# A hybrid decoder layer on one core: the order of each engine's instructions, made by the frame's other machine model

## The chip, the cores and the metric

The kernel runs on one core of one Trainium2 chip. The metric is the device time of one execution in microseconds (us), lower is better. The five engines that matter are TensorE (PE, with its weight loads shown apart as PEld), VectorE (DVE), ScalarE (ACT), GpSimd (POOL) and SyncE (SP), whose queue issues the transfers here. Every engine carries out its own list of instructions in order; engines wait for one another through semaphores.

## The reference, cut to what matters

One layer on 1024 tokens of width 1024, all in float32:

```python
h = h + 0.5 * swiglu(rmsnorm(h, ffn1_norm), w_gate, w_up, w_down)          # D_FF = 2816
z = rmsnorm(h, mix_norm) @ w_in
m_qk, m_v, m_o, m_if, f_q, f_k, f_v, f_f = split(z)
m_qk = silu(causal_depthwise_conv(m_qk, conv_qk))
h_m = mlstm_chunkwise(heads(m_q), heads(m_k), heads(m_v), i_gate, f_gate)  # 4 heads, a state carried from chunk to chunk
y_m = head_rmsnorm(h_m, mlstm_out_norm) * sigmoid(m_o)
h_f = forgetting_attention(heads(f_q), heads(f_k), heads(f_v), f_gate)     # 8 heads, causal softmax, "FoX"
y_f = head_rmsnorm(h_f, fox_out_norm)
h = h + concat([y_m, y_f]) @ w_out
h = h + 0.5 * swiglu(rmsnorm(h, ffn2_norm), ...)
gate = sigmoid(rmsnorm(h, ple_gate_norm) @ w_ple_gate)
h = h + gate * rmsnorm(p @ w_ple_proj, ple_proj_norm)
return rmsnorm(h, final_norm)
```

## The kernel before, in words

**Arithmetic.** Every large product is made of three products of float32r halves (`mm3`, L94 to L98: hi by hi, lo by hi, hi by lo). A number is split into its halves by `split_from` (L100 to L103): a cast on ScalarE gives hi, a subtraction on VectorE (or GpSimd) gives lo. A product tile is 128 rows by 512 columns, one PSUM bank.

**Stages, in the order of the program.** (1) p @ w_ple_proj (`pp` in `ple_rows`, `ph`/`pl` are the halves of p) beside the first norms. (2) The first SwiGLU: its up and gate products `pp` in a Winograd form of seven block products for each of 11 pairs of dff tiles, then its down products `dn`. (3) The mixer's projections and gates, then the mLSTM (`mlstm`, L831 to L1010), chunk by chunk of 128 tokens: `d` (L921, L924) and its exponential `E` on ScalarE (L927), `st` (L935) and `PT`, the two pairs of heads `num` (L951, L953), the update `dl` of the state `C` (L956, L964), then the norm: `dn`, `sq`, `ss`, `r` (GpSimd, L107), `ysb` (L981). `back` (L1000) transposes the finished heads. A chunk's `num` needs the state of the chunk before. PSUM has two buffers for `num`, one for `d` and `dl` together. (4) FoX (`fox`, L1026 to L1257): scores `sc` (L1111 to L1114), their maximum `mx`, the exponential `pr` (ScalarE, L1123), transposes `tr` (L1161) and their halves `th`/`tl` (L102, L103), value products `ot` (L1141), the sum `O` (L1148, L1149); for each pair of heads and half of the tokens `finish` (transposes L1193, `sq`, `ss`, `v`, `r`, `yn`, transposes L1211), and `put_y` (L1013 to L1023) stores the halves into `yD` in DRAM. (5) `out_f` (L1287 to L1306) loads `yfh`/`yfl` from `yD` (L1295) and adds their products with w_out to `h`. (6) The second SwiGLU, and `embed` (`g` products, sigmoid, final norm).

**What sets the order.** The code is written in the wanted order. `weave(main, fill, frac)` (L605 to L622) emits two generators so that `fill` gets `frac` of the TensorE time that `main` counts: the mLSTM chunks are woven with the projection of the output gate (`pj`, L1010, 0.9), the attention with the projections of the later head pairs and `out_m` (`acc`, L1257, 1.13). Products of `fill` need nothing that `main` has just made; below they are called filler. `later`/`tick` put a value product three steps behind its transposes. What the code emits is collected by the frame, `tile.TileContext` (L1507), which places buffers and semaphores and then makes the list of each engine by a model of the machine: an instruction is put where the model finds it ready, so the lists can differ from the code's order. In the kernel before, TensorE's list follows the code nearly row by row. SP's queue carries all loads and stores of the kernel.

Of the kernel before, what the change touches and what calls it, by code (L numbers as in the profile page):

```python
# [14 lines left out]
PSUM = bass.MemoryType.PSUM  # L15
# [9 lines left out]
# pairs of dff tiles, and the order of the seven block products of a Winograd form  # L25
# [4 lines left out]
class Net:  # L30
# [26 lines left out]
    def raw_cols(self, w, c0):  # L57
        """128 columns of a [1024, N] weight: row k * 128 + p at [p, k]."""
        r = self.rp.tile([P, KT, P], F32, tag="raw", name="raw")
        self.nc.sync.dma_start(out=r, in_=w[:, c0:c0 + P].rearrange("(k p) n -> p k n", p=P))  # L60
        return r
# [6 lines left out]
    def split(self, raw, pool=None, tag="w", aside=False):  # L68
        """raw = hi + lo, both in float32r."""
        pool = pool or self.wp  # L70
        shape = list(raw.shape)
        hi = pool.tile(shape, F32R, tag=tag + "hi", name=tag + "hi")
        lo = pool.tile(shape, F32R, tag=tag + "lo", name=tag + "lo")
        self.split_from(hi, lo, raw, aside)
        return hi, lo

    def split2(self, raw, aside=False):
        """The two halves of k of a weight tile, each (hi, lo)."""
# [14 lines left out]
    def mm3(self, out, ahi, alo, bhi, blo, first, last):  # L93
        """out (+)= a.T @ b with a = ahi + alo and b = bhi + blo."""  # L94
# [5 lines left out]
    def split_from(self, hi, lo, src, aside=False):  # L100
        """src (PSUM or SBUF) = hi + lo; aside: on GpSimd (SBUF only)."""
# [8 lines left out]
    def norm_rows(self, src, gain, dst):  # L110
        """dst = RMSNorm(src) * gain for 128 tokens; dst also takes the squares."""
# [7 lines left out]
    def xunit(self):  # L119
        """Four k tiles by 512 columns, (hi, lo)."""  # L120
        return tuple(self.xp.tile([P, 4, 512], F32R, tag=t, name=t) for t in ("xhi", "xlo"))

    def new_xt(self):
        """[half of the tokens][half of the k tiles] -> (hi, lo)"""
        return [[self.xunit() for _ in range(2)] for _ in range(2)]

    def normer(self, src, gain, dst):
        """RMSNorm of one token tile after another, transposed and split into dst(i) -> (hi, lo).
        Returns step(i), which takes token tile i and finishes the one before; step.rows(i) only takes it,
        step.next() only finishes the oldest."""  # L130
# [31 lines left out]
    def wino_put(self, B, name, rows, i):  # L162
        """512 columns of token tile i, transposed, into a right operand."""
# [10 lines left out]
    def wino_normer(self, src, gain, B, rows, bufs):  # L174
        """RMSNorm of one token tile after another into the right operands of the seven products
        (x transposed: rows k < 512 and k >= 512, columns t < 512 and t >= 512, Winograd's form).
        Three operands wait in DRAM for wino_rest. step(i) takes token tile i and finishes the one
        before, step.last() finishes the last."""
# [43 lines left out]
    def wino_rest(self, B, name):  # L222
        """One of the operands that wait in DRAM, through its place for lo."""
# [9 lines left out]
    def swiglu(self, B, w_gate, w_up, pools):  # L233
        """hidD = silu(x @ w_gate) * (x @ w_up), transposed, by pairs of dff tiles; the products of a
        pair (2 x 2 blocks: dff tile, half of k, half of the tokens) in Winograd's form with seven
        block products, each of three float32r products."""
# [3 lines left out]
        def pair(m, which, s):  # L240
            """Appends the seven products of the dff tiles m, m + 1."""
# [13 lines left out]
            # the first pair's tile a is loaded again for the sums  # L255
# [18 lines left out]
            def slot(r, c):  # L274
                """Where block (dff tile r, token half c) is put together."""
# [7 lines left out]
            def out(r, c, x, y, t):  # L283
                """Block (r, c) is x + y."""
# [8 lines left out]
            def hidden(r, c):  # L293
                """The left operands of the product with w_down: A11 = H00, A12 = H10, A21 = H01, A22 = H11
                (H: dff tile, half of the tokens), S1 = A21 + A22, S2 = S1 - A11, S3 = A11 - A21, S4 = A12 - S2."""
# [58 lines left out]
            # block (0, 0) = P1 + P2, (0, 1) = P1 + P6 + (P5 + P3), (1, 1) = P1 + P6 + P7 + P5,  # L354
            # (1, 0) = P1 + P6 + P7 + P4 (T4 is negated)
# [3 lines left out]
        for m in range(0, DFF // P, 2):  # L359
            s = {}  # L360
            g, u = pair(m, 0, s), pair(m, 1, s)
            # the first products don't need the second half of the tokens, those after them not T2, T3, T4
# [20 lines left out]
    def down(self, h, w_down, hook):  # L383
        """h += 0.5 * hid @ w_down in Winograd's form (2 x 2 blocks: half of the tokens, parity of the dff
        tile, half of the columns), one of the seven products after the other. Yields after the first loads
        and after the first operands; hook(j, q) runs after pair q of product j (the last one in two parts,
        4 and 8, of 256 tokens each)."""
# [20 lines left out]
        def fetch(j, q):  # L408
            """The left operands of two pairs."""
# [11 lines left out]
        def prep(n):  # L421
# [19 lines left out]
            # in place: T1 = B12 - B11, T3 = B22 - B12, T2 = B22 - T1, T4 = B21 - T2  # L441
# [18 lines left out]
        with tc.tile_pool(reuse_waits="tile", name="dn", bufs=1, side="right") as dn, \  # L460
# [11 lines left out]
            def evict(j, i):  # L472
                """Returns what can wait."""
# [18 lines left out]
            # C11 = P1 + P2, C12 = P1 + P6 + P5 + P3, C22 = P1 + P6 + P7 + P5, C21 = P1 + P6 + P7 + P4  # L492
            # (T4 is negated)
# [22 lines left out]
    def ffn(self, h, gain, w_gate, w_up, w_down, norms, hook, bufs, early=False, release=None):  # L516
        """h += 0.5 * SwiGLU(RMSNorm(h)); norms(step, prepare, products, pools, load_gain) runs the normalization
        over the token tiles, prepare() has the first weights split; early: products(n) may run there."""
# [39 lines left out]
    def ple_rows(self, p, w_proj, ps):  # L558
        """ppD = p @ w_proj; yields after every product of 128 tokens by 512 columns."""
# [45 lines left out]
def weave(main, fill, frac):  # L605
    """Emit main and fill so that they advance together: fill gets frac of main's TensorE time.
    Both yield that time in us, or None where the one has to wait for the other."""
# [17 lines left out]
def proj_stream(N, w, xt, jobs, bank=None, begun=None, aside=False):  # L625
    """jobs: (column or raw tile, sink(half, psum), ready or None); the weights are split one tile ahead.
    begun: the weights of the first job, whose first half is done (its sink gets None)."""
# [34 lines left out]
class Mix:  # L662
# [5 lines left out]
    def consts(self, pool):  # L668
        """Masks, selectors and the per-channel parameters as columns."""
# [9 lines left out]
        # rows 0-15: conv taps (tap, tile), 16-19 mlstm_out_norm, 20-23 fox_out_norm  # L679
# [9 lines left out]
    def begin(self, xt):  # L689
        """The gates and the first projection for the first half of the tokens, into DRAM; yields  # L690
        after the weights and then between products."""
# [24 lines left out]
    def gates(self, xt, keep, gp, bank):  # L716
        """Yields between its steps, with about the time that VectorE takes."""
# [17 lines left out]
        # log sigmoid(x) = min(x, 0) - ln(1 + exp(-|x|))  # L735
# [6 lines left out]
        # sums within chunks of 128  # L742
# [8 lines left out]
        # mLSTM rows 0-3: m, r = b - m, e = i - b  # L751
# [15 lines left out]
        # hi rows at 0-3, lo rows at 32-35, zeros between: one product with a 0/1 selector adds them  # L767
# [20 lines left out]
        # token-major: [:, chunk, (e, ws, exp(-m)), head]  # L788
# [8 lines left out]
        # FoX: c = sum over all tokens so far  # L797
# [19 lines left out]
        # selectors: sel[:, h, :] has ones in rows h and 32 + h; selp[:, pair, :] per 64 columns  # L817
# [13 lines left out]
    def mlstm(self, xt, keep):  # L831
        nc, N = self.nc, self.N
        with ExitStack() as ctx:
# [67 lines left out]
            def main():  # L901
                # winter = exp(b + m_prev - m), broadcast over the 64 rows of each head
# [15 lines left out]
                for c in range(NCH):  # L918
# [20 lines left out]
                    # keys, token-major, weighted for the state  # L939
# [571 lines left out]
```

## Time and profile before

| what | value |
|---|---|
| median of 3 runs | 2029.75 us (2027.75 to 2033.62) |
| span of the profiled execution | 2033.1 us |
| PE busy | 98% of the span, 9251 matmul records |
| PEld, DVE, ACT, POOL busy | 80%, 69%, 42%, 7% |

The profiled execution is told by its span, from the first to the last instruction; its own total isn't listed apart. The span lies 3.35 us above the median of the three runs and 0.5 us below the slowest of them, so a difference worked out on the span is laid on the median as it stands. A matmul's record begins when it is issued and lasts about 0.39 us, while the next one begins 0.23 us later: so "busy" says only that some matmul was under way, and it is the distance between starts that tells the rate.

### The profile page before, as it was taken

Reading aid. Unit: us, or ns where it says so; the run is one execution under the profiler, and the core shown is the slowest. Engines: PE = TensorE matmul, PEld = TensorE weight load, DVE = VectorE, ACT = ScalarE, POOL = GpSimd, SP = SyncE. Lnnn points to the kernel's source line nnn. Section 1 sums busy time; section 2 is a strip of 40 time slices with the busy share of each in tenths; the row PEclk is TensorE's granted clock in tenths of the full one; section 3 lists DMA queues with packets and bytes.
Section 4 is the critical chain, followed back from the end, with each engine's and each line's share of the span. In section 5 each row is a group of like instructions: output and inputs, shape, how many; then the busy total and the mean of one; then the engine's idle time right before and its main releaser. Section 6 shows DMA issues by size and latency. Waiting matters only on the chain. (4 is left out here: it accounts for less than half of the span.)

```text
span 2033.1 us, 25588 instructions
## 1 busy us (share of the span) xinstructions
PE 1982.7 (98%) x9251; PEld 1618.8 (80%) x9251; DVE 1408.4 (69%) x2425; ACT 856.9 (42%) x1634; POOL 135.9 (7%) x148
## 2 busy tenths in 40 slices
PE   7999999999999999999999999999999999999998
PEld 6788888888888787788788777788888888888786
DVE  6966766777877683655565665877777777886766
ACT  6433333334445443435565642433333333444443
POOL 2000000000000110121110411100000000000011
PEclk9999999999999999999999999999999999999999
DMA  7623322338432331122112538533223237633422
GB/s 284 207 89 104 112 96 95 104 112 310 149 101 99 111 86 53 42 95 53 53 54 78 190 122 289 197 106 112 94 94 124 89 99 243 234 104 102 131 70 86
DMA packets 205359, 252.62 MB, mean 124 GB/s; under 512 B 12632, under 2 KB 138096, under 8 KB 204464
## 3 DMA queue, kind: packets, MB, share of 16 engines
q1 hardware_dynamic: 205232, 250.99, 37.8%
q8 instruction: 72, 1.18, 0.2%
q14 instruction: 55, 0.45, 0.1%
HBM read 172.18 MB, written 74.58 MB: 121 GB/s over the span
## 5 line engine op out<-in xcount | busy, mean ns | idle before, releaser
L96 PE MATMUL pp<-xhi,whi 128*128 128x512 f32 x704 | 275.6, 391 | 0.5 <-DVE s L272 0.5
L98 PE MATMUL pp<-xhi,wlo 128*128 128x512 f32 x704 | 274.1, 389 | 0.8 <-DVE wlo L103 0.8
L97 PE MATMUL pp<-xlo,whi 128*128 128x512 f32 x704 | 274.7, 390 | 0.0
L102 ACT CAST whi<-raw 128x512 fp32r<-128x512 f32 x180 | 111.3, 621 | 257.4 <-PE pp L97 177.2
L102 ACT CAST whi<-S 128x512 fp32r<-128x512 f32 x176 | 109.5, 622 | 240.8 <-PE pp L97 186.2
L96 PE MATMUL dn<-xhi,whi 128*128 128x512 f32 x528 | 205.7, 390 | 0.1
L97 PE MATMUL dn<-xlo,whi 128*128 128x512 f32 x528 | 205.5, 389 | 0.0
L98 PE MATMUL dn<-xhi,wlo 128*128 128x512 f32 x528 | 205.1, 389 | 0.0
L102 ACT CAST whi<-ar 128x512 fp32r<-128x512 f32 x132 | 82.3, 623 | 183.3 <-PE dn L97 174.8
L98 PEld LDWEIGHTS pp<-xhi,wlo 128*128 128x128 f32 x704 | 132.3, 188 | 29.2 <-DVE wlo L103 1.2
L96 PEld LDWEIGHTS pp<-xhi,whi 128*128 128x128 f32 x704 | 132.3, 188 | 29.1 <-DVE s L272 0.8
L97 PEld LDWEIGHTS pp<-xlo,whi 128*128 128x128 f32 x704 | 132.3, 188 | 27.7 <-DVE xlo L103 0.3
L103 DVE TENSOR_TENSOR wlo<-raw,whi 128x512 fp32r<-128x512 f32 x162 | 110.5, 686 | 59.7 <-ACT whi L102 46.7
L103 DVE TENSOR_TENSOR wlo<-S,whi 128x512 fp32r<-128x512 f32 x176 | 120.1, 682 | 25.8 <-ACT whi L102 25.7
L103 DVE TENSOR_TENSOR wlo<-ar,whi 128x512 fp32r<-128x512 f32 x132 | 90.7, 687 | 63.9 <-ACT whi L102 63.8
L96 PEld LDWEIGHTS dn<-xhi,whi 128*128 128x128 f32 x528 | 99.1, 188 | 21.0 <-DVE t L272 0.5
L98 PEld LDWEIGHTS dn<-xhi,wlo 128*128 128x128 f32 x528 | 99.1, 188 | 20.7
L97 PEld LDWEIGHTS dn<-xlo,whi 128*128 128x128 f32 x528 | 99.1, 188 | 20.6
L272 DVE TENSOR_TENSOR p<-pp,p 128x512 f32<-128x512 f32 x88 | 60.6, 689 | 74.9 <-PE pp L98 74.9
L107 POOL TENSOR_TENSOR r<-v,mhalf 128x1 f32<-128x1 f32 (+1 forms) x56 | 43.9, 784 | 909.6 <-DVE v L116 756.1
L96 PE MATMUL pj<-xhi,whi 128*128 128x512 f32 x248 | 102.6, 414 | 0.1
L97 PE MATMUL pj<-xlo,whi 128*128 128x512 f32 x248 | 97.5, 393 | 0.0
(350 smaller groups left out, 4515.0 us busy)
## 6 DMA issues: line engine op xcount, KB each, us to landing
ar<-hidD SPq DMA_DIRECT2D x60, 512.0 KB, 3.6
hidD<-t SPq DMA_DIRECT2D x110, 256.0 KB, 3.4
raw<-in_ffn_w_gate_dram SPq DMA_DIRECT2D x46, 512.0 KB, 3.9
raw<-in_ffn_w_up_dram SPq DMA_DIRECT2D x46, 512.0 KB, 3.7
raw<-in_w_in_dram SPq DMA_DIRECT2D x24, 512.0 KB, 3.9
hidD<-x SPq DMA_DIRECT2D x44, 256.0 KB, 3.1
ar<-hidD SPq DMA_DIRECT2D x32, 256.0 KB, 2.9
w<-in_ffn_w_down_dram SPq DMA_DIRECT2D x8, 1024.0 KB, 11.1
```

Source lines behind the costliest of these rows:

```text
L96: mm(out, ahi, bhi, start=first, stop=False)
L97: mm(out, ahi, blo, start=False, stop=False)
L98: mm(out, alo, bhi, start=False, stop=last)
L102: self.nc.scalar.copy(out=hi, in_=src)
L103: (self.nc.gpsimd if aside else self.nc.vector).tensor_tensor(out=lo, in0=src, in1=hi.bitcast(F32), op=ALU.subtract)
L107: self.nc.gpsimd.tensor_tensor(out=r, in0=v, in1=self.mhalf[:, :v.shape[-1]], op=ALU.pow)
L272: add = lambda d, x, y: nc.vector.tensor_tensor(out=d, in0=x, in1=y, op=ALU.add)
```

## The change

One line of `kernel`; the other lines of the difference take out comments and docstrings and keep the line numbers.

```diff
-    with tile.TileContext(nc) as tc:
+    with tile.TileContext(nc, schedule_with_timeline_sim=True) as tc:
         layer(tc, *args, out)
```

The frame then asks another model of the machine, one that keeps a timeline of each engine, when an instruction is ready. The instructions, tiles, buffers and data are the same in number and kind: 9161 rows on TensorE, 2427 on VectorE, 618 on SyncE; of ScalarE's loads of a table of functions one stands before another line. Only the place of rows in the five lists differs: 3808 of TensorE's rows, 1388 of VectorE's, 678 of ScalarE's, 256 of SyncE's and 21 of GpSimd's stand elsewhere. In the two SwiGLU bodies TensorE's order is the same row for row and VectorE's differs by two or three places; in the down products by up to 20 places; in the mixer, between the mLSTM and `out_f`, rows stand 30 to 140 places from where they were on the average.

The first place is TensorE's list in the mLSTM, from the last products of chunk 4 to the first of chunk 5 (`pj` is the filler). Before:

```order
L951 MATMUL num_7306<-C1_6733,qw_6022 128x258
L953 MATMUL num_7306<-v1_6020,PT_7247 128x129 x2
L956 MATMUL dl_7310<-v1_6020,kw_7265 128x258
L96 MATMUL pj_7286<-xhi_5528,whi_7039 128x512
L97 MATMUL pj_7286<-xlo_5529,whi_7039 128x512
L98 MATMUL pj_7286<-xhi_5528,wlo_7040 128x512
...
L921 MATMUL d_7333<-ident_r_5371,mask_r_5378 128x512
L924 MATMUL d_7333<-R_6213,sel_6387 128x128 x4
```

and after:

```order
L951 MATMUL num_7306<-C1_6733,qw_6022 128x258
L953 MATMUL num_7306<-v1_6020,PT_7247 128x129 x2
L956 MATMUL dl_7310<-v1_6020,kw_7265 128x258
L951 MATMUL num_7367<-C0_6732,qw_6022 128x258
L1000 MATMUL tr_7497<-ident_75,ysb_7174 128x128
L921 MATMUL d_7333<-ident_r_5371,mask_r_5378 128x512
L924 MATMUL d_7333<-R_6213,sel_6387 128x128 x4
L1000 MATMUL tr_7513<-ident_75,ysb_7174 128x128 x2
L956 MATMUL dl_7371<-v1_6020,kw_7362 128x258
```

The `pj` rows between the chunk's own rows are gone. From `dl_7149` (chunk 3) to `pj_7642` (the first FoX projection) the list before has 136 rows between, 3 to 9 `pj` in each gap between dependent rows; the list after has 47 rows and no `pj`. Those `pj` stand earlier, in blocks of 20 to 24 between the rows of chunks 0 to 3.

The second place is the end of FoX on TensorE: `tr_10891` and `tr_10926` are transposes of the normalised output of the last head pair, `tr_10910` those of the last `O`, `acc_10906` and `acc_10947` products of `out_m` (filler). Before:

```order
L1211 MATMUL tr_10891<-ident_75,yn_10830 128x128 x4
L96 MATMUL acc_10906<-xhi_10020,xhi_10018 128x512
...
L1193 MATMUL tr_10910<-ident_75,O_10094 128x128 x4
...
L96 MATMUL acc_10947<-xhi_10022,xhi_10018 128x512
L97 MATMUL acc_10947<-xlo_10023,xhi_10018 128x512
L1211 MATMUL tr_10926<-ident_75,yn_10924 128x128 x4
L98 MATMUL acc_10947<-xhi_10022,xlo_10019 128x512
```

and after, down to the first products of `out_f`:

```order
L1141 MATMUL ot_10790<-th_10864,V_9502 128x256
L1211 MATMUL tr_10891<-ident_75,yn_10830 128x128 x4
L1141 MATMUL ot_10790<-tl_10865,V_9502 128x256
L1141 MATMUL ot_10790<-th_10864,V_9502 128x128
L1141 MATMUL ot_10790<-tl_10865,V_9502 128x128
L1193 MATMUL tr_10910<-ident_75,O_10094 128x128 x4
L1211 MATMUL tr_10926<-ident_75,yn_10924 128x128 x4
L96 MATMUL acc_11066<-wf_10212,yfh_11057 128x512
L97 MATMUL acc_11066<-wf_10213,yfh_11057 128x512
L96 MATMUL acc_11080<-wf_10212,yfh_11057 128x512
```

All products of `out_m` now stand ahead of the last 171 rows of FoX (in matmuls, rows 5464 to 5634 of the unfolded list), and the first products of `out_f` directly follow the last transposes.

The third place is SP's queue at the same point (`th`, `tl` into `yD` are the stores of the last FoX outputs, `yfh`/`yfl` the loads of `out_f`, `hr` into `hD` the stores of `out_m`, `raw_11184` and `raw_11190` the first weights of the second SwiGLU). Before:

```order
L1022 DMA yD_83<-th_10931 128x512
L1023 DMA yD_83<-tl_10932 128x512
L1284 DMA hD_82<-hr_10904 128x1024
L1295 DMA yfh_11057<-yD_83 128x4x512
L1295 DMA yfl_11058<-yD_83 128x4x512
L1284 DMA hD_82<-hr_10962 128x1024
L1295 DMA yfh_11061<-yD_83 128x4x512
L1284 DMA hD_82<-hr_10993 128x1024
L1295 DMA yfl_11062<-yD_83 128x4x512
```

and after:

```order
L1284 DMA hD_82<-hr_10993 128x1024
L60 DMA raw_11184<-in_ffn2_w_gate_dram 128x8x128
L60 DMA raw_11190<-in_ffn2_w_up_dram 128x8x128
L1022 DMA yD_83<-th_10547 128x512
L1023 DMA yD_83<-tl_10548 128x512
L1022 DMA yD_83<-th_10896 128x512
L1023 DMA yD_83<-tl_10897 128x512
L1022 DMA yD_83<-th_10931 128x512
L1023 DMA yD_83<-tl_10932 128x512
L1295 DMA yfh_11057<-yD_83 128x4x512
L1295 DMA yfl_11058<-yD_83 128x4x512
```

The stores of `out_m` and two weight loads now come ahead of the last stores into `yD`, and the loads of `out_f` follow these with nothing between.

## The prediction

> **What bounds the kernel now.** The page comes first: its shares of busy time, then the same by stages.
>
> ```profile
> span 2033.1 us, 25588 instructions
> PE 1982.7 (98%) x9251; PEld 1618.8 (80%) x9251; DVE 1408.4 (69%) x2425; ACT 856.9 (42%) x1634; POOL 135.9 (7%) x148
> ```
>
> TensorE is the bound. How full it is differs by stage; the windows of equal length show it (length, then PE, PEld, DVE, ACT and POOL busy us with records, granted clock, DMA share, GB/s):
>
> ```profile
> 100.00:150.00 50.00, 50.00 (x219) 40.84 (x218) 34.73 (x55) 17.40 (x29) 0.00 (x0) 1.00 0.30 95
> 800.00:850.00 50.00, 49.80 (x256) 37.10 (x255) 28.22 (x96) 17.39 (x42) 5.59 (x8) 1.00 0.08 22
> 931.00:1212.00 281.00, 264.55 (x1505) 217.67 (x1503) 175.78 (x385) 161.27 (x415) 50.74 (x34) 0.99 0.29 89
> 1150.00:1200.00 50.00, 47.98 (x285) 39.05 (x283) 36.30 (x84) 29.89 (x81) 6.44 (x3) 1.00 0.41 137
> ```
>
> In the SwiGLU (100 to 150) TensorE never rests, and in the mLSTM (800 to 850) it rests 0.2 us of 50. In FoX (931 to 1212) it rests 281 − 264.55 = 16.45 us. So an order can win in FoX, around it and at the two ends of the kernel; in the SwiGLU and the mLSTM it can only lose. The waits of the weight loads from 930 to 1215 say for whom FoX rests (total, times, longest):
>
> ```profile
> PEld sc L1111 <- ACT pr L1123: 10.7, 22, 1.2
> PEld ot L1141 <- DVE O L1149: 7.7, 14, 1.6
> PEld tr L1161 <- DVE tl L103: 3.5, 7, 0.7
> PEld tr L1161 <- DVE yn L1204: 3.0, 2, 2.2
> ```
>
> These are waits on semaphores by dependent work that stands a little early in the list. Their sum is 24.9 us; part of it lies under matmuls still running, since TensorE itself rests only 16.45.
>
> **The change part by part.** No work is added or removed, so each term is a wait that appears or goes. Where no filler stands, I take the serial chain from its rows, less the matmuls that remain beside it.
>
> *SwiGLU, 0.* TensorE's rows keep their order there, and VectorE's move by two or three places. VectorE is busy 34.73 of 50 us and TensorE 50.00, so the slack covers the shift; there is nothing to gain. If that cover failed by one 0.69 us piece in each of the 22 passes (11 pairs, two SwiGLUs), it would cost 15 us.
>
> *Start, −3.* ScalarE's list now has `ph` ahead of the big casts of weights:
>
> ```profile
> 5.77 1.04 ACT L102 CAST wp0hi<-raw 128x1024 fp32r<-128x1024 f32 x1 [3.76 <-DMA raw<-in_w_ple_proj_dram]
> 9.27 0.36 ACT L102 CAST ph<-tr 128x256 fp32r<-128x256 f32 x1
> 9.69 0.79 PE L96 MATMUL pp<-wp0hi,ph 128*128 128x512 f32 x1 [6.10 <-ACT ph L102]
> ```
>
> The first product then needs only `wp0hi`, ready at 6.81, rather than `ph`, ready at 9.63: 2.8 us. Bounds −3 and 0, should the weights' second half be late instead.
>
> *mLSTM, +12.* The filler is gone from the hops of chunks 4 to 7. What it covered is in these rows of one chunk:
>
> ```profile
> 842.02 0.61 PE L953 MATMUL num<-v,PT 128*128 128x129 f32 x4
> 842.47 0.60 PE L956 MATMUL dl<-v,kw 128*128 128x258 f32 x2
> 843.14 0.70 DVE L964 SCALAR_TENSOR_TENSOR C<-C,dec,dl 64x129 f32<-64x129 f32 x2
> 845.44 0.42 DVE L981 TENSOR_TENSOR ysb<-num,r 128x256 f32<-128x256 f32 x1 [0.88 <-POOL r L107]
> 851.84 0.58 ACT L883 COPY G<-pj 128x512 f32<-128x512 f32 x1
> 852.44 1.28 ACT L885 ACT_TABLE_LOAD   x1
> 853.73 1.91 ACT L885 ACTIVATE G<-G 128x2048 f32<-128x2048 f32 x1
> 860.64 1.28 ACT L927 ACT_TABLE_LOAD   x1
> ```
>
> `num` ends at 842.63 and its bank is free when `ysb` ends, at 845.86: 3.2 us. Both banks of `num` are held by the two pairs of a chunk, so a bare chunk takes 3.2 us and the 1.2 us in which its own `num` products run, 4.4 in all. The rows that stay in the bare stretch (16 of L953, 12 of L935, 6 each of L951 and L956, 12 of L924, 3 of L921, 12 transposes) take about 14.8 us at the distances of starts in this trace, for example (842.47 − 842.02)/2 = 0.22 for one L953: 3.7 for each of four chunks. That leaves 0.7 each, +2.8. The sigmoid's copy, table load, work and table load back (0.58 + 1.28 + 1.91 + 1.28 = 5.05 us) now fall ahead of `E` of chunk 4, with about 1.4 us beside them: +3.6. The last L1000 transposes wait for the last `ysb`, bare: the same 3.2. And `d` must wait for the one bank that `dl` leaves after two 0.70 us updates, part of it beside the chain above: +2. Together 11.6, taken as +12. If all but the chain of the banks and the sigmoid hide, it is +6; if the two pairs of each chunk run one after the other (another 4 × 2 us), +20. What is queued behind the waiting rows is the whole rest of the mixer.
>
> *FoX ahead of its tail, −8.* About 22 us of projections are pulled ahead of the scores, and more filler stands between dependent rows there. All of the 24.9 us above can go at most. Against it, a hop with under a microsecond between the release and its use is as frequent in the new list as in the old, so some waits return. Between 0 and −25 I take half of what TensorE visibly rests, 8 of 16.45.
>
> *FoX tail, +8.* That pull has a price: the last 171 matmul rows of FoX now stand without filler. Their matmuls go at these distances:
>
> ```profile
> 1119.97 0.60 PE L1161 MATMUL tr<-ident,pr 128*128 128x128 f32 x4
> 1120.32 0.36 PE L1141 MATMUL ot<-th,V 128*128 128x256 f32 x1
> 1120.52 0.28 PE L1141 MATMUL ot<-tl,V 128*128 128x256 f32 x1
> ```
>
> 0.09 to 0.20 us each, some 20 us in all. The same rows bring 68 VectorE instructions; at the mean of the window from 1150 (36.30/84 = 0.43) that is 29 us. VectorE becomes the bound of this stretch: +9 if it works through, less what it has done ahead; +8. Bounds 0 (VectorE catches up under the earlier filler) and +14 (each also waits for ScalarE).
>
> *The last normalisation, +4.* The chain of waits shows it, start and length:
>
> ```profile
> 1208.36 0.61 ACT sq L1195
> ...
> 1210.02 1.65 POOL r L107
> 1211.69 0.70 DVE yn L1204
> ...
> 1212.44 0.66 PE L1211 MATMUL tr<-ident,yn 128*128 128x128 f32 x4 [1.59 <-DVE yn L1204]
> ```
>
> From 1208.36 to 1212.44 is 4.1 us. Before, TensorE rested for the last 1.59 of it, with filler beside the rest; after, it rests for all of it (the 1.59 of before are taken off below). Bounds +2, if the value products before it end late, and +5.
>
> *Start of out_f, +10.* The loads need the last stores of `yD`, which need the last `tr`:
>
> ```profile
> 1214.63 0.58 SPq L1023 DMA_DIRECT2D yD<-tl  x1
> 1216.57 0.37 SPq L1295 DMA_DIRECT2D yfh<-yD  x1
> ...
> 1231.73 5.91 SPq L60 DMA_DIRECT2D raw<-in_ffn_w_up_dram  x1
> ...
> 1227.96 0.50 PE L98 MATMUL acc<-wf,yfl 128*128 128x512 f32 x1 [1.21 <-DMA yfl<-yD]
> ```
>
> From the last transposes (1212.44) to the first product with `yfl` (1227.96) is 15.5 us, and filler runs beside nearly all of it. In the new list only eight products with `yfh` (1.8 us) are there. The stores of `out_m` are out of the queue's way now, so I take 12 for the same path, less 1.8: +10. Lower end: 4.1 us (1212.44 to 1216.57) to the issue of `yfh` and as much again for it to land, +6; upper end 15.5 − 1.8 = 13.7, and if SP's row for the second weights stalls for its buffer as it does at 1231.73 (5.91), with the stores queued behind it, 19.
>
> *Waits of before that go there, −5*: the 1.59 us ahead of `tr`, the 1.21 ahead of `acc`, and the longest wait on `yn` of the list above, 2.2; bounds −3 and −5. *After out_f, −2*: the last `dn` and first `g` products wait here,
>
> ```profile
> PE dn L98 <- DVE v L116: 1.5, 1, 1.5
> PE g L96 <- ACT gwhi L102: 0.8, 1, 0.8
> ```
>
> and the transposes of the normalised rows stand ahead of the last `dn` now. Bounds 0 and −2.3.
>
> Sum: −3 + 12 − 8 + 8 + 4 + 10 − 5 − 2 = **+16**, 2049 on the span and 2046 on the median.
>
> A rule of the Trainium skill would add to this ("TensorE: Matmul & The Clock Gate", Part 1: The HAM clock gate): after an idle window of about 3.4 us the array falls to half its clock until it has been busy about as long. It would make the bare waits cost more than their length. The trace's own rows for it come among the rivals.
>
> **The rivals.** (a) *Faster.* FoX's waits all go (−23, with the 2.2 of `yn` counted once) and the bare stretches cost their lower ends: −3 + 6 − 23 + 4 + 2 + 6 − 5 − 2 = −15, 2015 on the median. For it: 24.9 us of waits, each short (at most 2.2 us), which a row's place can remove. Against: TensorE rests only 16.45 us.
>
> (b) *Near equal.* FoX gives its 16.45, and the losses are −3 + 8 + 4 + 3 + 8 − 5 − 2 = +13: −3, 2027. For it: the mLSTM's own rows run beside each other where I laid them end to end. This is also the case in which the lists' difference changes nothing that TensorE feels; with 3808 of its rows moved, I give that no chance of its own.
>
> (c) *Slower through the rate of products after the bare waits.* After its first 6 us of idle time TensorE issues at half rate for a while:
>
> ```profile
> 10.28 0.63 PE L97 MATMUL pp<-wp0lo,ph 128*128 128x512 f32 x1
> 10.70 0.63 PE L96 MATMUL pp<-wp0hi,ph 128*128 128x512 f32 x1
> 13.54 0.65 PE L98 MATMUL pp<-wp0hi,pl 128*128 128x512 f32 x1
> 14.03 0.40 PE L96 MATMUL pp<-wp1hi,ph 128*128 128x512 f32 x1
> 14.27 0.40 PE L97 MATMUL pp<-wp1lo,ph 128*128 128x512 f32 x1
> ```
>
> 0.42 us between starts until 13.54, and 0.24 from 14.03 on. A wait that long elsewhere would be followed by 3.5 us at that rate, a loss of 3.5 × (1 − 0.24/0.42) = 1.5 us. It decides from a wait as long as that one; nothing in FoX or the mLSTM waits so long before. If the wait at `out_f`, the sigmoid's, the last `ysb` and the last normalisation each bring it, that is +6: 2052. The rule of the Trainium skill above agrees with these rows in the halved rate and its length.
>
> (d) *Slower through the mLSTM alone*: pairs in turn, +20 instead of +12, with SP's stall: 2046 + 8 + 6 = 2060. It is the top of my own case.
>
> **How the numbers follow.** My own case, with (d) as its top, gets 0.53 and runs from 2036 to 2062; (c) 0.12; (a) 0.19; (b) 0.16. A measurement of this kernel can tell 0.3%, 6 us, from no change, so the first two are slower (0.65), (a) is faster and (b) the same. The predicted time is 2046. The range goes from 2012, a little below (a), to 2070, which takes in the slower ends of `out_f` and of the mLSTM at once but not with 15 us in the SwiGLU.
>
> **What would show it.** Right: TensorE waiting on `yfh` or `yfl` at `out_f` for some 10 us; gaps of 2 to 4 us on `num` and `d` between the sixth and the last chunk of the mLSTM, with ScalarE's table load before `E` among them; in the tail of FoX a DVE busier than PE; FoX's waits on `pr` and `O` about half of now. Wrong: if FoX ahead of its tail is shorter by 15 us or more, or its tail keeps TensorE busy, the sign turns; if the SwiGLU windows show PE under 49.9 of 50, the cover that I counted on isn't there. That the waits appear but are shorter than the chains above would bring it down to (b).

## The result and the profile after

| | before | after |
|---|---|---|
| median | 2029.3 us | 2076.9 us (2075.52 to 2078.2, 4 runs) |
| ratio, 95% interval | 1 | 1.0229 (1.0215 to 1.0242) |
| span of the profiled execution | 2033.1 us | 2076.4 us |

The change makes the kernel slower by 47 us. The sign was forecast, and so were the places; the size was 16 us, and 2076.9 lies outside the range of 2012 to 2070. The medians and ratios below leave out two slow executions, one of fox_leash20 (2803.92 us at a granted clock of 0.654) and one of the kernel before (2184.72 us at 0.85).

The page of the changed kernel, its first lines and the granted clock in 40 slices (tenths of the full TensorE clock):

```profile
span 2076.4 us, 25633 instructions
PE 1999.1 (96%) x9251; PEld 1639.5 (79%) x9251; DVE 1402.2 (68%) x2425; ACT 855.5 (41%) x1634; POOL 137.0 (7%) x148
PEclk9999999999999999989999988999999999999999
```

The work is the same, record for record. TensorE rests 77.3 us of its span against 50.4 before (2076.4 − 1999.1, 2033.1 − 1982.7), its records are 16.4 us longer in all, and two dips stand in the clock that before doesn't have. To find the stages, the starts of TensorE's row of the same number are compared in both traces, at numbers ahead of which the two lists hold the same rows. At three of them (3373, 3891, 4070) the row itself is another one:

| up to the start of | before, us | after, us | difference | of this stage |
|---|---|---|---|---|
| row 248, the last transposes ahead of the first SwiGLU | 66.0 | 63.2 | −2.8 | −2.8 |
| row 2239, among the down products of the first SwiGLU | 517.6 | 517.5 | −0.1 | +2.7 |
| row 3373, the mLSTM's values | 771.5 | 771.7 | +0.2 | +0.3 |
| row 3891, the mLSTM's end | 892.4 | 910.9 | +18.5 | **+18.3** |
| row 4070, where FoX's scores begin in the list of before | 931.1 | 951.3 | +20.2 | +1.7 |
| row 5635, `out_f` | 1226.1 | 1265.0 | +38.9 | **+18.7** |
| row 7790, the down products of the second SwiGLU | 1716.4 | 1756.4 | +40.0 | +1.1 |
| row 8753, among the `g` products | 1936.3 | 1980.9 | +44.6 | **+4.6** |
| end of the span | 2033.1 | 2076.4 | +43.3 | −1.3 |

The stages add up to 43.3 and not to the 47.6 of the medians: the span of the changed kernel lies 0.5 us below its median, that of the kernel before 3.8 us above 2029.3.

Within FoX the two lists have no common point, so I count there how far TensorE's starts lie apart beyond what is usual for their kind, which is an estimate: from row 4070 to the first row of the tail (row 5464) 38.8 us before and 28.5 after, −10.3; from there to `out_f` 5.5 before and 34.4 after, +28.9. The profile of before is slow just here. In a run told below, pe_before, TensorE has the same list row for row, and the two stretches take 256.7 and 33.5 us there, against 259.6 and 35.4 in the profile of before. So of the −10.3 some 3 us are not the change's, and the tail's loss is nearer to 31.

The windows of the changed kernel, with the columns of the prediction's, for the SwiGLU, the last chunks of the mLSTM, FoX ahead of its tail, and the tail:

```profile
100.00:150.00 50.00, 50.00 (x219) 40.79 (x218) 34.92 (x56) 17.55 (x30) 0.00 (x0) 1.00 0.30 95
872.00:911.00 39.00, 30.18 (x135) 23.06 (x134) 22.39 (x84) 14.73 (x32) 5.54 (x8) 0.82 0.13 41
951.00:1210.00 259.00, 249.17 (x1394) 210.93 (x1393) 147.59 (x328) 136.68 (x354) 40.98 (x29) 0.99 0.31 97
1210.00:1251.00 41.00, 30.32 (x171) 25.13 (x169) 30.41 (x65) 25.47 (x65) 7.98 (x4) 0.83 0.18 56
```

The SwiGLU is as full as before. In the two bare stretches TensorE rests 9 and 11 us, and no other engine is full either: VectorE is busy 22.39 of 39 and 30.41 of 41 us. That is what a chain looks like in which one engine hands over to the next. The granted clock is 0.82 and 0.83 there: of the 39 and the 41 us some 14 each passed at half the clock. TensorE's waits there (total, times, longest), first for 872 to 915, then for 1210 to 1266:

```profile
PE dl L956 <- ACT E L927: 3.7, 2, 2.8
PE tr L1000 <- DVE ysb L981: 2.6, 1, 2.6
PE d L921 <- DVE C L964: 2.1, 3, 0.9
PE num L951 <- DVE ysb L981: 0.4, 1, 0.4
```

```profile
PE acc L96 <- DMA yfh<-yD: 8.2, 1, 8.2
PE tr L1161 <- DVE tl L103: 5.4, 8, 1.6
PE tr L1211 <- DVE yn L1204: 4.6, 2, 4.2
PE sc L1111 <- ACT pr L1123: 2.6, 4, 0.8
```

FoX ahead of its tail shows the other side, the waits of the weight loads that the prediction listed, from 951 to 1210:

```profile
PEld sc L1111 <- ACT pr L1123: 4.4, 11, 0.9
PEld ot L1141 <- DVE O L1149: 2.5, 4, 1.0
PEld tr L1161 <- DVE tl L103: 1.1, 2, 0.8
```

Before, ahead of the tail (930 to 1190), these were 10.3, 7.2 and 2.8; the prediction's 10.7, 7.7 and 3.5 run to 1215 and take in its tail.

The end of the second SwiGLU has a wait that I hadn't forecast. TensorE's timeline there (start, length):

```profile
1941.62 0.39 PE L97 MATMUL dn<-w,ah 128*128 128x512 f32 x1
1946.65 1.22 PE L98 MATMUL dn<-w,al 128*128 128x512 f32 x2 [4.64 <-DVE al L103]
1947.67 0.63 PE L96 MATMUL dn<-w,ah 128*128 128x512 f32 x1
1948.09 0.63 PE L97 MATMUL dn<-w,ah 128*128 128x512 f32 x1
...
1952.69 0.39 PE L96 MATMUL dn<-w,ah 128*128 128x512 f32 x1
1952.92 0.39 PE L97 MATMUL dn<-w,ah 128*128 128x512 f32 x1
```

The products with `ah` have been pulled ahead, then `al` isn't there; after 4.64 us of rest starts lie 0.43 us apart until 1952.

### The profile page after: what moved, and what is told of

The parts are those of the page before. It is cut to its first block, busy times and chain, and to the rows that moved or that the text cites. A ratio compares the mean times of both kernels' runs of the same rounds, so it can differ in the third digit from the quotient of the medians.

```text
span 2076.4 us, 25633 instructions
## 1 busy us (share of the span) xinstructions
PE 1999.1 (96%) x9251; PEld 1639.5 (79%) x9251; DVE 1402.2 (68%) x2425; ACT 855.5 (41%) x1634; POOL 137.0 (7%) x148
## 4 chain that ended last, share of the span: by engine, by line
PE 61%; DVE 6%; DMA 3%; ACT 3%; issue 1%; POOL 1%; SPq 0%; POOLq 0%; ACTq 0%; DVEq 0%
PE pp L96 6%; PE pp L97 6%; PE pp L98 6%; PE dn L98 6%; PE dn L96 6%; PE dn L97 6%; PE acc L98 3%; PE acc L96 3%; PE acc L97 3%; PE pj L96 3%; PE pj L97 2%; PE pj L98 2%; PE tr L1161 1%; PE ot L1141 1%; DMA t<-ppD 1%
## 5 line engine op out<-in xcount | busy, mean ns | idle before, releaser
L96 PE MATMUL dn<-xhi,whi 128*128 128x512 f32 x528 | 189.5, 389 | 1.3 <-DVE t L272 1.3
```

What stands on the lines that cost most here:

```text
L96: mm(out, ahi, bhi, start=first, stop=False)
```

## The experiments

In all of them the computation is that of the kernel; in two, products that nobody reads are added. Each ratio is to the kernel before, run beside it on the same chip. `pin` in the diffs adds edges that fix the order of an engine's list and nothing else.

**1. Holding TensorE to the code's order, stage by stage.**

```diff
+    mark(tc, "mlstm")
     ... M.mlstm(xt, keep)
+    mark(tc, "fox")
...
         layer(tc, *args, out)
+        pin(tc)     # PINNED = {"PE": ("mlstm",)}; {"PE": ("late fox",)}; {"DVE": ("late down",)};
+                    # {"PE": ("mlstm", "late fox", "late down"), "DVE": ("late down",)}
```

The first was expected to do this:

> The changed kernel, with TensorE's list held to the code's order in the mLSTM alone, so that the output-gate products stand between the dependent rows of chunks 4 to 7 again. Theory A (the loss is in TensorE's lists, stage by stage, and each stage's loss stands alone): the 18.5 us that the mLSTM lost (21 us from 890 to 911 where before took 2) come back, 2058 us, and the granted clock from 880 to 920 us goes from 0.7 to 1.00. Rival B (the lists of the other engines, made with TensorE's, cost the time, or what one stage gets back the next one loses): 2070 us or more.

2071.9 us, ratio 1.0212 (1.0196 to 1.0229): 5 us came back, not 18.5, though the granted clock from 880 to 920 is 1.00 again, as expected. It falls elsewhere, to 0.57 from 810 to 820.

> The changed kernel, with TensorE's list held to the code's order from the seventh head of FoX to the first products of out_f, so that products of out_m stand in the tail again. Theory A: the tail's loss (28.9 us against before between row 5464 and the first product of out_f, with 8.5 us of waiting for yfh in it) goes, and of the 10.3 us that FoX ahead of it had won some 3 go too: 2051 us. Rival B: the wait for yfh stays at 8 us or the tail stays bound by VectorE: 2065 us or more.

2071.55 us, 1.021 (1.0191 to 1.023): 5 us, not 26. The wait for `yfh` is gone; in the late FoX `ot` now waits for `O`, 6.1 us in all.

> The changed kernel, with VectorE's list held to the code's order from the seventh block product of the second SwiGLU's down stage on. Theory A (the 4.6 us wait for al at 1946 us, and the 14 products at 0.43 us each behind it, come from VectorE's list, where three subtractions for the next gate weights and updates of h stand ahead of al): the wait goes, 2070 us. Rival B (TensorE's list, with the hi products pulled ahead, causes it): 2077 us, the wait stays.

2077.07 us, 1.0243 (1.022 to 1.0266). Neither theory: the wait for `al` was gone (TensorE's waits from 1935 to 1965 are four on `w`, 3.4 us in all), and nothing came of it.

> All three together, with TensorE's list in the late down stage held too; the order of the other model is left in the start, the first SwiGLU, FoX up to the sixth head, and on the other engines. Theory A (the losses add up): 2077 - 18 - 26 - 7 = 2026 us, at or a little below the kernel before, with about 7 us won in FoX. Rival B: above 2040 us.

2063.39 us, 1.0167 (1.0146 to 1.0187). Theory A as it stood had fallen: the losses don't come back with the code's order. The profile of the first run says why for the mLSTM, in its waits of TensorE from 770 to 930:

```profile
PE pj L96 <- ACT G L883: 4.3, 5, 1.3
PE wd L907 <- ACT wb L909: 2.6, 3, 1.1
PE tr L878 <- ACT vt L870: 2.2, 2, 1.2
```

The filler itself waits, for its one bank: in the code a group of `pj` follows the one before at once, and the new group can't start until ScalarE has copied the old one to `G`. The kernel before doesn't have this wait; in its list chunk rows stand in between. "TensorE follows the code nearly row by row" hid that the few short moves mattered.

**2. Lists of before, row for row.**

```diff
+LISTS = {"PE": "0-1 4-5 10-11 6-9 2-3 12-19 ..."}      # places in the code's order, as in the kernel before
+        pin(tc)
```

> The changed kernel with TensorE's list held, row for row, to that of the kernel before; the other four lists come from the other model, which sees TensorE's list as given. After holding TensorE to the code's order in the mLSTM and late FoX brought back only 14 of 47 us, two theories. C: the code's order isn't the order of before (which moves 789 rows by a place or two, so that chunk rows stand between one bank of pj and the next); with before's own list the mLSTM's and the FoX tail's losses go and only what VectorE's list costs at the end of the second SwiGLU stays, 7 us: 2037 us. B: ScalarE's and VectorE's lists of the other model bring the waits: 2055 us or more.

2028.74 us, ratio 1.0 (0.9991 to 1.001). With TensorE's list put back, the whole loss is gone. The other four lists were made anew for it: of VectorE's rows 982 stand elsewhere than in the kernel before and 928 elsewhere than in the changed one.

> The other way round: VectorE's, ScalarE's, SyncE's and GpSimd's lists are held to those of the kernel before, TensorE's comes from the other model given these. C: TensorE's list alone carries the loss, so 2065 us or more. B: the other lists carry it, so 2040 us or less.

2145.54 us, 1.0576 (1.056 to 1.0592). So a TensorE list of the other model is enough for a loss, and to hold TensorE's list is enough to undo it; where the other lists are fixed, the model makes an even worse one. The changed kernel's own TensorE list beside the four lists of before wasn't run.

**3. One stretch of TensorE's new list at a time.** The list of before, with the rows 3373 to 3948, 3948 to 5635, or 7790 to 8753 as in the changed kernel.

> The changed kernel with TensorE's list of the kernel before, except for the rows from the first value projection of the mLSTM to the first projections of FoX, which stand as the other model put them; the other four lists come from the other model, which sees this list as given. If the loss adds up stage by stage in TensorE's list: the 18.5 us that these rows lost, 2047 us. If what this stage loses depends on what stands before and behind: under 2040 us.

2056.51 us, 1.0127 (1.011 to 1.0145).

> The same with FoX and out_m alone as the other model put them (up to the first product of out_f). Adding up: 10 us won ahead of the tail, 29 lost from the tail's first row to the first product of out_f, 2048 us, with a wait for yfh of 8 to 9 us. If the tail's loss came from the other lists: 2035 us or less.

2060.54 us, 1.0149 (1.0134 to 1.0164); its waits for `yfh` are 8.5 us and for `yfl` 2.5.

> The same with the end of the second SwiGLU's down products alone as the other model put them. Adding up: one wait of 4 to 5 us for al and a dozen products at 0.43 us behind it, 2036 us. If VectorE's list caused that wait: no wait and 2029 us.

2029.95 us, 1.0006 (0.9996 to 1.0017): neither the 2036 of adding up nor a run without the wait. The wait is there, 4.4 us in one piece, against 1.9 in pe_before, so TensorE's own rows lengthen it. From row 7790 to 8753 the run is 4.4 us longer than the profile of before, but pe_before is 3.3 us longer there too. The wait is worth about 1 us, and the time doesn't move.

The mLSTM costs 27 us and FoX 31, more than the 18.3 and 18.7 seen in the changed kernel. Two stretches make the loss, and they don't add up: 57 alone, 47 together. The profiles say where the 10 us lie. From row 3373 to 3891 seg_mlstm takes 146.2 us and the changed kernel 139.2; from `out_f` to row 7790 seg_fox takes 495.8 and the changed kernel 491.4. In both places the run with the longer time also has more of it at half the clock, 30.7 against 13.7 us and 11.6 against 5.0. What the half clock costs is taken up below.

**4. Bare rows without the other model.** The kernel before, with filler used up early by the weave, and then with unread products in the bare rows.

```diff
-            weave(main(), fill, 0.9)
+            weave(main(), fill, 1.8)               # bare; bare_dummy: fill, then for the rest of main:
+                    for _ in range(3):
+                        nc.tensor.matmul(dm, self.ident_r, xt[0][0][0][:, 0, :], start=True, stop=True)
...
-            weave(attention(), fill(), 1.13)
+            weave(attention(), fill(), 1.6)        # bare_fox; bare_fox_dummy as above
```

> The kernel before, with its own machine model, and only the share of filler in the mLSTM changed (0.9 to 1.8), so that the output-gate products are used up after chunk 4 and the last chunks stand bare, as in the changed kernel. If bare chunks alone cost what the mLSTM lost: +15 to +19 us, 2046 us, with a granted clock of about 0.7 there. If the other lists were needed for the loss: +8 us or less, 2037 us.

2038.4 us, 1.0048 (1.0033 to 1.0063): +10, between the two forecasts, at a clock of 0.91 and not 0.7.

> The run named bare, and once the filler is used up 128x512 products that nobody reads are woven into the bare chunks, about 16 us of them at full rate; nothing waits for them. Theory K (a third to a half of the loss in the bare stretch is TensorE at half rate after idle time): more work makes it faster, the stretch keeps a clock of 1.00 and the kernel comes out 4 to 9 us below bare. Theory L (the loss is the length of the chain on the other engines alone): the same time as bare, or up to 10 us more.

2045.44 us, 1.0082 (1.0065 to 1.0098), as theory L had it. The windows of the bare chunks, of bare and of bare_dummy:

```profile
867.00:905.00 38.00, 30.12 (x158) 22.56 (x159) 26.76 (x93) 16.59 (x36) 8.62 (x11) 0.91 0.24 83
```

```profile
867.00:905.00 38.00, 36.28 (x202) 27.93 (x202) 26.28 (x91) 15.60 (x34) 7.70 (x11) 1.00 0.19 65
```

44 more matmuls at the full clock, and FoX's first scores begin at 940.0 us in the one and 940.6 in the other. Either the half rate, 6.8 us long in bare, costs next to nothing there, or the added products cost as much as the full clock gives back; the run can't tell the two apart. In these two profiles 4 us of the difference come after the mLSTM.

> The kernel before, with its own model, and only the share of filler in FoX changed (1.13 to 1.6), so that the last 200 or so rows of FoX stand without products of out_m. If bare rows alone cost what the tail lost: out_f waits 8 us or more for yfh, the tail is 15 us or more longer, in all 2050 us. If TensorE's other moves were needed: under 2040 us.

2057.36 us, 1.0135 (1.012 to 1.0149): +27. The waits of TensorE from 1195 to 1255:

```profile
PE acc L96 <- DMA yfh<-yD: 8.4, 1, 8.4
PE tr L1211 <- DVE yn L1204: 5.3, 2, 4.5
PE tr L1161 <- DVE yn L1204: 2.8, 1, 2.8
```

The first two are also among the changed kernel's three largest, here with the old model. Missing filler is enough for the tail's loss.

> The run named bare_fox, with 128x512 products that nobody reads woven into the bare rows once out_m is used up; nothing waits for them. Theory K (a good part of the tail's loss is TensorE's half rate after idle time): the clock there is 1.00 and the kernel comes out 4 us or more below bare_fox, though it does more. Theory L (the chain between the engines is what takes the time): the same time as bare_fox or up to 10 us more.

2062.44 us, 1.016 (1.0144 to 1.0176). `out_f` begins at 1247.3 us, in bare_fox at 1247.1; but the last filler begins at 1192.6, in bare_fox at 1195.2, so the bare stretch is 2.8 us longer, 54.7 against 51.9. The windows of the tail, of bare_fox and bare_fox_dummy:

```profile
1195.00:1235.00 40.00, 28.20 (x167) 23.81 (x165) 26.82 (x62) 21.91 (x58) 5.18 (x3) 0.86 0.17 60
```

```profile
1195.00:1235.00 40.00, 34.46 (x200) 29.57 (x200) 26.71 (x61) 21.69 (x58) 2.60 (x2) 0.91 0.14 50
```

Theory L again by its time. The clock didn't reach the 1.00 of theory K; over the whole bare stretch it is 0.85 against 0.78. So 33 more matmuls in this window win nothing, and what the half clock alone costs in the tail stays open.

**5. Short moves only.** TensorE may not issue an instruction ahead of one that stands 20 (or 10) places before it in the list of the kernel before.

```diff
+        for n in range(1, len(row)):        # row: TensorE's list of the kernel before
+            first = n - 1 if not FOX[0] < n < FOX[1] else max(n - LEASH, FOX[0])
...
+            tc.add_manual_dep(row[n], row[first].name, ...)
```

> The changed kernel, in which no instruction of TensorE may run ahead of one that is 20 places before it in the list of the kernel before: the other model orders freely within that reach, and filler cannot be used up early. Theory D (the gain lies in short moves, the loss in long ones): about 7 of the 10 us won in FoX stay and the tails are covered, 2022 us. Theory E (any filler that is pulled out of a gap is missed there): 2030 us or more.

Here the reach holds for the whole list. 2029.55 us, 0.9997 (0.9988 to 1.0007), just short of theory E's 2030. Beside the profile of before FoX was 12 us shorter, the mLSTM 6 longer.

> The changed kernel with TensorE's list of the kernel before outside FoX; inside FoX and out_m the other model orders freely, but no instruction runs ahead of one 20 places before it. In the run leash20 FoX was 12 us shorter than before and the mLSTM 7 us longer, the end of the second SwiGLU 2 to 5. Theory D (FoX's gain comes from short moves and stands by itself): 2029 - 12 + 2 = 2019 us. Theory E (what FoX gains is lost behind it, at out_f and in the SwiGLU): 2026 us or more.

2026.76 us, the median of seven, 0.998 (0.997 to 0.9991): theory E.

> The same with a reach of 10 places. If the waits that go are those of one row just ahead of its time (1 to 2 us, five to ten products): nearly all of the gain stays, 2021 us. If longer moves are needed: 2026 us or more.

2036.0 us, 1.0024 (1.0015 to 1.0033): the gain doesn't stay, and the kernel is a little slower than before. `out_f` begins 8.6 us earlier than in the profile of before, and the second SwiGLU's first product only 2.2 us earlier: what FoX wins is lost right behind it. So the shorter reach and the end of FoX aren't told apart here.

> The kernel of fox_leash20 once more, for a profile. If what FoX gains is lost behind it: FoX ahead of out_f 8 to 12 us shorter than before, and 6 us or more of that lost between the first product with yfh and the second SwiGLU's first product, where yfl and the loads of h are waited for.

TensorE's waits of that profile from 1180 to 1300:

```profile
PE acc L96 <- DMA yfh<-yD: 3.8, 1, 3.8
PE acc L98 <- DMA yfl<-yD: 2.9, 1, 2.9
```

The last transposes of FoX are 9.7 us earlier than in the profile of before (1203.1 against 1212.8; 5.4 us earlier than in pe_before), but less filler is left to cover the stores and loads behind them: 30 rows of TensorE against 58. `out_f` begins 12.1 us earlier, as expected; but only 2.7 of them are lost by the second SwiGLU's first product, not 6 or more, and another 2.4 by row 7790.

> The same, with the reach of 20 places only up to row 5400 of TensorE's list; from there on, and so in the tail and at out_f, it is row for row that of the kernel before. If the end of FoX gave back what its middle had won: 2020 us or less. If the gain is bound by when the last stores and loads of FoX land, whatever the list: 2025 us or more.

2022.23 us, 0.9962 (0.9948 to 0.9976), between the two forecasts. With the last rows of before, the waits are

```profile
...
PE tr L1211 <- DVE yn L1204: 1.6, 1, 1.6
...
PE acc L98 <- DMA yfl<-yD: 0.4, 1, 0.4
```

and the gain in FoX stays: from row 4070 to 5464 TensorE takes 247.3 us, in pe_before 256.7. This version beats both kernels, by 8 us and 55 us.

## Why the prediction was right in sign and wrong in size

**Start, −3.** Right: `ph` is cast at 3.56 us and the first product begins at 6.60.

```profile
3.56 0.37 ACT L102 CAST ph<-tr 128x256 fp32r<-128x256 f32 x1 [1.55 <-PE tr L565]
6.60 1.22 PE L96 MATMUL pp<-wp0hi,ph 128*128 128x512 f32 x2 [3.08 <-ACT wp0hi L102]
```

But the 2.8 us were gone at row 2239, among the first down products. I took a gain at the start for a gain at the end without asking whether the stages behind it had slack; which row took it back I haven't traced.

**SwiGLU, 0.** Right for its body. At its end the term "after out_f, −2" had the wrong sign, +4.6 − 1.3: I counted which waits of before would go, and not what comes late once the products with `ah` are ahead of `al`. The runs seg_down and pe_before show that the wait for `al` is worth about 1 us and that 3.3 of the 4.6 us come with TensorE's old list too; what they are isn't settled.

**mLSTM, +12.** The place and the mechanism were right: `E` late behind the sigmoid (the 2.82 us ahead of `dl` at 885.88, after table loads at 878.72 and 883.39), `d` behind `C`, the last transposes behind `ysb` (2.60).

```profile
877.11 0.60 PE L956 MATMUL dl<-v,kw 128*128 128x258 f32 x2
878.72 1.28 ACT L885 ACT_TABLE_LOAD   x1
880.01 1.91 ACT L885 ACTIVATE G<-G 128x2048 f32<-128x2048 f32 x1
883.39 1.28 ACT L927 ACT_TABLE_LOAD   x1
884.68 1.14 ACT L927 ACTIVATE E<-d,tok 128x128 f32<-128x128 f32 x4
885.88 1.23 PE L956 MATMUL dl<-v,kw 128*128 128x258 f32 x2 [2.82 <-ACT E L927]
```

The size was 18.3, and half of it is no rest of TensorE. From row 3373 to 3891 it rests 9.8 us against 0.5 before, and its busy time grows by 9.0 us. One reason is a term that my sum put at nothing, the clock. From 884.2 to 894.4 the granted clock is 0.50; from 885.88 on TensorE waits for nothing there, and a `dl` of two records takes 1.23 us where it took 0.60 at 877.11. Three kernels have the same five lists in this stage. Their windows from row 3373 to 3891, of the changed kernel, of pe_latefox and of dve_latedown:

```profile
771.71:910.88 139.17, 129.36 (x612) 101.73 (x610) 59.73 (x192) 47.38 (x92) 11.05 (x16) 0.95 0.14 38
```

```profile
769.67:907.38 137.71, 128.24 (x611) 100.73 (x610) 59.72 (x192) 47.42 (x92) 11.05 (x16) 0.96 0.14 39
```

```profile
772.37:916.37 144.00, 135.29 (x611) 105.89 (x610) 59.80 (x193) 47.42 (x92) 11.13 (x16) 0.89 0.13 37
```

TensorE rests 9.8, 9.5 and 8.7 us in them, nearly the same; but 13.7, 10.2 and 32.3 us pass at half the clock, and the stage is the longer the more of that it has. The last two differ by 6.3 us of time and 22.1 us at half clock, 0.28 us for each; by this estimate some 4 of the 18.3 us are the clock's, and the other 14 lie near my 12. The run bare, which has the missing filler and not the new list's other moves, cost 10 with 6.8 us at half clock. What those other moves cost isn't separated.

**FoX ahead of its tail, −8.** Right: −10.3, or some 7 beside pe_before, from the waits I had named.

**Tail, +8, last normalisation, +4, out_f, +10, less 5.** Together +17, measured +28.9. Two of them were near: 4.17 us ahead of the last transposes, 8.2 ahead of `yfh`. **The step that failed is the tail's cadence.** I set it to VectorE's busy time less TensorE's, 29 against 20. VectorE's work came out as counted, 30.41 us, but the tail took 41 us and then the normalisation: 21 us over TensorE's 20, where I had 8. That is about the 12 us missing here. I treated two engines as two parallel piles of work of which the larger decides; without filler they are links of one chain (`pr`, transposes, `tl`, `ot`, `O`), in which TensorE rests 10.7 of the 41 us while others work. The run bare_fox shows that missing filler alone brings it: from its last filler to the first product with `yfh` it takes 51.9 us, the changed kernel 54.4 from row 5464. Of the 41 us some 14 pass at half the clock. How much of the price is the handing over and how much the clock, no run separates: bare_fox_dummy has a higher clock and a stretch 2.8 us longer.

**Rival (c), half rate after a wait.** The rate is real: 0.43 us between starts after the wait for `al`, above, and after the wait for `yfh`:

```profile
1264.96 0.79 PE L96 MATMUL acc<-wf,yfh 128*128 128x512 f32 x1 [8.23 <-DMA yfh<-yD]
1265.56 0.63 PE L97 MATMUL acc<-wf,yfh 128*128 128x512 f32 x1
1265.98 0.63 PE L96 MATMUL acc<-wf,yfh 128*128 128x512 f32 x1
```

At these two places, where much work follows, 12 and 7 starts lie 0.2 us too far apart, 2.4 and 1.4 us. In the mLSTM it costs some 4 us more by the estimate above, so with the tail left open it comes to some 8 us, where (c) had 6: a part of the loss, as (c) had it, beside the bare waits. Its condition was too strict: it asked for a wait as long as the 6 us at the start, and in the mLSTM the clock halved with no wait above 2.8 us, after 3.4 us in which TensorE was busy for 1.36 (880.8 to 884.2). The rule of the Trainium skill ("TensorE: Matmul & The Clock Gate", Part 1: The HAM clock gate) names an idle window of about 3.4 us ahead of the halving and a busy one of about that length ahead of the full clock. The rest of 4.64 us at 1942 agrees with it; the half rate behind it held for longer, from 1946.65 to 1952.69.

**Rival (d)**, the mLSTM at +20, was nearer to its 18.3 than my own term. **Rivals (a) and (b)** were wrong in the full kernel, but their mechanism exists: with the reach of moves limited and the end of FoX fixed, what FoX gains outweighs the rest. In the sum of (a) I also took +4 for the tail, whose lower end I had set at 0; with 0 it comes to −19.

**What I weighed wrongly beside the sum.** I spoke of filler as something that covers waits, and put a price on each wait by itself. But filler is a fixed stock. What the model pulled forward to win some 7 to 10 us was missing at the end of the mLSTM and of FoX, and there the whole length of the chain shows. Nor had I a term for the clock, which is 0.82 and 0.83 in the bare stretches and 1.00 in the SwiGLU.

## What to carry to other kernels

A list scheduler that issues whatever is ready spends independent work early, and dependent work at the end of a stage then stands bare: before trusting a better machine model, look at how much independent work each stage has left for its last chain. To price a bare stretch, lay the chain end to end; the larger of the engines' busy times is only its lower bound (30 us of VectorE in a tail of 41). Then look at the clock granted in it: the same lists took 137.7 to 144.0 us in three kernels. And limiting how far an instruction may move to 20 places, with the last rows of a stage fixed, kept the gain (0.9962) and none of the loss. With the end of the stage free as well, 20 places gave 0.998 and 10 places 1.0024; 10 places with the end fixed weren't run.

## What the runs showed that I had not expected

- One engine's list decides: with TensorE's of before and the four others by the other model the ratio is 1.0; with the four of before and TensorE's by the other model it is 1.0576.
- The code's own order is not the list of before: held to it in three stages, the kernel keeps 34 of the 47 us. A group of filler that follows its forerunner at once waits for its bank (five times in the mLSTM, 4.3 us in all).
- TensorE took 44 extra matmuls in the bare chunks of the mLSTM, and FoX's scores began 0.6 us later; in FoX's tail it took 33 in the window shown, and the bare stretch grew by 2.8 us.
- The same lists don't give the same time: in the mLSTM three kernels with equal lists there took 137.7, 139.2 and 144.0 us, in step with the time at half the clock.
